# Pinned instruction order, operand tiles made ahead and moved pools in a hybrid decoder layer

## The chip, the cores and the metric

The kernel runs on one core of one Trainium2 chip. The metric is the device time of one launch in microseconds (us); the median of three runs of the kernel before is 2411.76 (2410.3 to 2414.46). TensorE (PE) multiplies matrices, PEld is its weight load, VectorE (DVE), ScalarE (ACT) and GpSimd (POOL) work on elements, SyncE (SP) starts loads. Each engine takes its instructions in the order in which they are queued.

## The reference

One decoder layer over 2048 tokens of 1024 features, all in float32; `D_FF` is 2816.

```python
h = rms_norm(x, g_mix[i])
proj = h @ w_in[i]
u, v, qk, vm, o, ig, fg = jnp.split(proj, cuts, axis=-1)
gm = gmlp_mixer(u, v, gm_ln_g[i], gm_ln_b[i], gm_ws[i], gm_bs[i])      # 8 heads, chunks of 128 tokens
qk = jax.nn.silu(causal_dwconv(qk, ml_conv_w[i], ml_conv_b[i]))
q, k = jnp.split(qk, 2, axis=-1)
ml = mlstm_mixer(q, k, vm, ig + ml_b_i[i], fg + ml_b_f[i], o, ml_norm_g[i])   # 4 heads, chunks of 128
x = x + jnp.concatenate([gm, ml], axis=-1) @ w_out[i]
h = rms_norm(x, g_ffn[i])
up = causal_dwconv(h @ w_up[i], ffn_conv_w[i], ffn_conv_b[i])
a, bv = jnp.split(up, 2, axis=-1)
x = x + (jax.nn.silu(a) * bv) @ w_down[i]
gate = jax.nn.sigmoid(rms_norm(x, g_ple[i]) @ w_ple_gate[i])
x = x + gate * (p[i] @ w_ple[i])
# after the layer: rms_norm(x, g_final)
```

## The kernel before

**Products.** Every large float32 product is made from operands that are split into a high part and the remainder, both in the type fp32r: high by high, high by low, low by high, so three matmuls for each pair of tiles. `wsplit`, `split` and `halves` make the parts: ScalarE copies the high part, VectorE subtracts it to get the low one. Features lie on the partitions and tokens along them.

**Mixer.** Four blocks of 512 tokens (`b` from 0 to 3). In a block `tok_group(0)` to `tok_group(3)` make the columns with tokens on the partitions (gates, v, o), `chain1` to `chain3` the running sums and maxima of the mLSTM gates, `qk_tile` the eight convolved tiles of q and k (steps `u`, `cv`, `qk`), `head_a`, `head_b` and `head_out` the mLSTM heads one after another (`hc` is scaled by `sr` at L588 to L591, transposed into `tr` at L598, and written to `cat`), `u_tile` and `mix` the gMLP heads. `out_first` starts two tiles of the output projection between the steps of the last head; the other six follow, 24 matmuls each, and each tile is added to `xr` (the input) and stored to `x1s`. While that runs, `split` makes the `h` of the next block from `hf` (L683), 8 times; the last block has none.

**Side work.** VectorE has work in the mixer that serves the channel mixer. `ffn_in` normalizes a finished block and stores it, and sums of it, to the DRAM tiles `tds`; `sums_make` (L261 on) adds and subtracts parts of `w_down` that `sums_load` has brought into the two tiles `ds0` and `ds1`, and stores the results to `sds`. In the program text most `sums_make` stand in the loop over output tiles, four of them in the last block.

**Channel mixer.** Two halves of 1024 tokens. Both its products use a scheme of seven products of half-size blocks in place of eight, in the order `ORDER = (1, 2, 6, 5, 7, 3, 4)`. `Up` makes 22 column tiles (`j`) from the tiles `T[prod, kk]`, 4 for each of the seven products, 28 in all, which `build_t` loads from `tds` and splits during `j = 0`; for the second half `load_t` and `make_t` do it during `Down`. `Down` (L940 to L1016) takes 11 steps for each product; its `load` (L952, L953) brings weights and activations into slots `x`, `prep` splits them (`dw`, `dt`, L770 and L771), `fetch` (L962) brings residuals that are needed when a product is complete. `sums` of `Up` (L912) stores the sums of activations that `Down` reads. A list of steps gives each load and each split a lead: `(4, load)` is issued four steps ahead of the matmuls that need it.

**Last stage.** `Ple` runs four blocks of gate products (`gt`, `gs`) with its weights loaded by `load4` (L1035) during the second `Down`. The last block goes in two halves of 256 tokens. For each, `q1` sums the squares by small matmuls and takes the root, `q2` spreads the scale `dgf` over the tokens (L203), and `emit_half` (L1130) multiplies the eight tiles by it and stores them.

**Order.** Loads are issued by SP, stores by POOL (two weight loads at the start by ACT). The framework chooses the order of each engine's instructions by a model of its own, so an instruction of later work may be queued ahead of what stands before it in the text. `tc.keep_in_program_order` (in `keep`) ties an instruction behind the one that was traced before it on the same engine. On-chip memory is handed out by pools in the order in which these are opened; `SLOTS` gives the tags of the channel mixer's slots, `(count, columns)`.

## Time and profile before

| | |
|---|---|
| median of the runs | 2411.76 us |
| profiled execution | 2413.49 us, span 2411.8, mean granted clock 0.99 |
| busy: PE / DVE / ACT / POOL | 2347.6 (97%) / 1814.7 (75%) / 1106.5 (46%) / 206.3 (9%) |
| mixer blocks 0 to 3 end at | 228.9, 448.7, 663.7, 884.6 us |
| first half: `Up` ends, `Down` ends | 1318.8, 1534.0 us |
| second half: `Up` ends, `Down` ends | 1956.1, 2147.0 us |
| `Ple` | 264.8 us, to the end of the span |

Busy time is the time in which an engine executes an instruction; the span runs from the first to the last recorded instruction, and the execution's own time is a little longer than the span. PE's busy share by stage goes from 94% (block 0, 216.02 of 228.90) to nearly 100% (second `Up`, 421.04 of 422.10). The granted clock is the share of TensorE's full speed that the chip gave in a stretch.

### The profile page before, as it was taken

Reading aid. Unit: us, or ns where it says so; the run is one execution under the profiler, and the core shown is the slowest. Engines: PE = TensorE matmul, PEld = TensorE weight load, DVE = VectorE, ACT = ScalarE, POOL = GpSimd, SP = SyncE. Lnnn points to the kernel's source line nnn. Section 1 sums busy time; section 2 is a strip of 40 time slices with the busy share of each in tenths; the row PEclk is TensorE's granted clock in tenths of the full one; section 3 lists DMA queues with packets and bytes.
Section 4 is the critical chain, followed back from the end, with each engine's and each line's share of the span. In section 5 each row is a group of like instructions: output and inputs, shape, how many; then the busy total and the mean of one; then the engine's idle time right before and its main releaser. Section 6 shows DMA issues by size and latency. Waiting matters only on the chain.

```text
span 2411.8 us, 31443 instructions
## 1 busy us (share of the span) xinstructions
PE 2347.6 (97%) x11336; PEld 1992.5 (83%) x11336; DVE 1814.7 (75%) x3107; ACT 1106.5 (46%) x1850; POOL 206.3 (9%) x339
## 2 busy tenths in 40 slices
PE   8999999999999989999999999999999999999998
PEld 8888977998798868878888788888888878888887
DVE  7787678668756859888988566888888866575665
ACT  4453266246315635444444565544444445553223
POOL 1000110011211100011100000010000000000000
PEclk9999999999999999999999999999999999999998
DMA  7426452644556454345435787332323368671112
GB/s 251 132 70 202 131 183 84 205 140 149 202 174 202 139 209 153 136 148 179 141 109 179 262 292 236 130 116 101 109 101 117 117 221 300 210 261 45 70 70 71
DMA packets 148413, 382.73 MB, mean 159 GB/s; under 512 B 17696, under 2 KB 19872, under 8 KB 148256
## 3 DMA queue, kind: packets, MB, share of 16 engines
q1 hardware_dynamic: 121872, 291.16, 37.1%
q0 software_dynamic: 26240, 89.15, 9.5%
q8 instruction: 89, 1.46, 0.2%
q14 instruction: 68, 0.56, 0.1%
q10 hardware_dynamic: 144, 0.40, 0.1%
HBM read 283.12 MB, written 97.52 MB: 158 GB/s over the span
## 4 chain that ended last, share of the span: by engine, by line
PE 81%; DVE 7%; DMA 6%; issue 3%; ACT 1%; POOL 1%; SPq 0%; DVEq 0%; POOLq 0%; ACTq 0%
PE ub L864 6%; PE ub L865 6%; PE ub L866 6%; PE ua L864 4%; PE ua L865 4%; PE ua L866 4%; PE acc L125 3%; PE acc L126 3%; PE gt L125 3%; PE gt L126 3%; PE gt L128 3%; PE da L977 3%; PE acc L128 3%; PE da L978 3%; PE da L976 3%; PE acc L369 3%
## 5 line engine op out<-in xcount | busy, mean ns | idle before, releaser
L864 PE MATMUL ub<-tt,sw 128*128 128x512 f32 x704 | 275.3, 392 | 7.4 <-ACT tt L770 4.6
L865 PE MATMUL ub<-tt,sw 128*128 128x512 f32 x704 | 275.2, 391 | 2.8 <-DVE tt L771 2.8
L866 PE MATMUL ub<-tt,sw 128*128 128x512 f32 x704 | 274.6, 390 | 0.0
L776 ACT ACTIVATE sw<-wr 128x1024 fp32r<-128x1024 f32 x132 | 140.1, 1061 | 289.2 <-PE ua L865 247.2
L864 PE MATMUL ua<-tt,sw 128*128 128x512 f32 x528 | 206.0, 390 | 0.0
L865 PE MATMUL ua<-tt,sw 128*128 128x512 f32 x528 | 205.9, 390 | 0.0
L866 PE MATMUL ua<-tt,sw 128*128 128x512 f32 x528 | 205.7, 390 | 0.0
L771 DVE TENSOR_TENSOR dt<-sx,dt 128x512 fp32r<-128x512 f32 x154 | 106.4, 691 | 105.1 <-ACT dt L770 104.8
L369 PE MATMUL acc<-whi,hh 128*128 128x384 f32 (+1 forms) x512 | 174.1, 341 | 8.5 <-ACT hh L218 7.0
L118 DVE TENSOR_TENSOR wlo<-wst,whi 128x1024 fp32r<-128x1024 f32 (+2 forms) x144 | 158.4, 1103 | 24.9 <-ACT whi L114 15.9
L370 PE MATMUL acc<-wlo,hh 128*128 128x384 f32 (+1 forms) x512 | 173.5, 339 | 2.6 <-DVE wlo L118 2.6
L371 PE MATMUL acc<-whi,hl 128*128 128x384 f32 (+1 forms) x512 | 173.0, 339 | 0.2 <-DVE hl L219 0.2
L777 DVE TENSOR_TENSOR sw<-wr,sw 128x1024 fp32r<-128x1024 f32 x132 | 161.2, 1221 | 15.1 <-ACT sw L776 12.3
L864 PEld LDWEIGHTS ub<-tt,sw 128*128 128x128 f32 x704 | 132.5, 188 | 38.5 <-ACT tt L770 5.5
L770 ACT ACTIVATE dt<-sx 128x512 fp32r<-128x512 f32 x154 | 96.9, 629 | 135.3 <-PE db L978 73.9
L865 PEld LDWEIGHTS ub<-tt,sw 128*128 128x128 f32 x704 | 132.7, 188 | 30.9 <-DVE tt L771 3.6
L866 PEld LDWEIGHTS ub<-tt,sw 128*128 128x128 f32 x704 | 132.7, 189 | 27.5
L976 PE MATMUL da<-dt,dw 128*128 128x512 f32 x352 | 137.0, 391 | 7.1 <-ACT dt L770 7.1
L977 PE MATMUL da<-dt,dw 128*128 128x512 f32 x352 | 138.1, 392 | 0.3 <-DVE dt L771 0.2
L978 PE MATMUL da<-dt,dw 128*128 128x512 f32 x352 | 137.7, 391 | 0.0
L114 ACT ACTIVATE whi<-wst 128x1024 fp32r<-128x1024 f32 x80 | 84.2, 1058 | 93.0 <-PE acc L371 35.2
L771 DVE TENSOR_TENSOR dw<-sx,dw 128x512 fp32r<-128x512 f32 x154 | 105.7, 686 | 24.2 <-ACT dw L770 24.2
(341 smaller groups left out, 5766.8 us busy)
## 6 DMA issues: line engine op xcount, KB each, us to landing
wr<-w_up SPq DMA_DIRECT2D x44, 512.0 KB, 3.6
wr<-w_up SPq DMA_DIRECT2D x88, 256.0 KB, 4.8
act<-fc POOLq DMA_DIRECT2D x44, 512.0 KB, 5.8
ad<-two POOLq DMA_DIRECT2D x88, 256.0 KB, 4.9
sx<-sd SPq DMA_DIRECT2D x88, 256.0 KB, 3.8
sx<-ad SPq DMA_DIRECT2D x88, 256.0 KB, 4.0
wst<-w_v SPq DMA_DIRECT2D x48, 384.0 KB, 3.4
sx<-w_down SPq DMA_DIRECT2D x66, 256.0 KB, 4.1
```

What stands on the lines that cost most here:

```text
L118: (leng or V).tensor_tensor(lo[:, :n], st[:, :n], hi[:, :n].bitcast(F32), ALU.subtract)
L369: PE.matmul(ps[t][:, :n], a_h, rh, start=(k == 0), stop=False)
L370: PE.matmul(ps[t][:, :n], a_h, rl, start=False, stop=False)
L371: PE.matmul(ps[t][:, :n], a_l, rh, start=False, stop=(k == KD - 1))
L771: keep(V.tensor_tensor(t[:, HALF:], x, t[:, :HALF].bitcast(F32), ALU.subtract), pin)
L777: keep(V.tensor_tensor(lo, x, hi.bitcast(F32), ALU.subtract), pin)
L864: PE.matmul(ps, hi[:, c], t[:, :HALF], start=first, stop=False, skip_group_check=on)
L865: PE.matmul(ps, hi[:, c], t[:, HALF:], start=False, stop=False, skip_group_check=on)
L866: PE.matmul(ps, lo[:, c], t[:, :HALF], start=False, stop=last, skip_group_check=on)
L976: PE.matmul(ps, w[:, c], t[:, :HALF], start=first, stop=False, skip_group_check=on)
L977: PE.matmul(ps, w[:, c], t[:, HALF:], start=False, stop=False, skip_group_check=on)
L978: PE.matmul(ps, w[:, HALF + d * 128:HALF + (d + 1) * 128], t[:, :HALF], start=False, stop=last, skip_group_check=on)
```

## The change

The edits, in the order of the diff:
- Slots `k` are divided into `kp` (12) and `k` (16). `kp` and the temporary and persistent pools of the mixer get places of their own: `big` and the new pool `pre` lie on the other side of the memory, `sm` and `tp` are opened earlier, tiles of 320 and 96 bytes (`GAP_W`, `GAP_P`) are put between, each tag of slots has its own pool. `xr` of the mixer has three buffers in place of two.
- The first weight load and the first load of the input are made in two halves each, and the first splits too.
- `keep` is put on VectorE instructions: `hf`, the first operation of `sums_make`, those of `ffn_in`, the scale in `q1`, `dgf` in `q2`, the products of `emit_half`; and on SP's loads in `load_t`, `fetch`, `load4` and `Ple.load`.
- The 12 tiles `T` of products 1, 2 and 6 of the first half are loaded and split during the last output projection (`pre_load`, `pre_make`); the other 16 are built as before, with a lead of 3 steps in place of 8.
- The last `sums` of an `Up` half uses slots `m` in place of `x`.
- In the end the first half's `emit_half` is cut in two, with the second half's `q2` between.

```diff
-SLOTS = {"k": (28, 1024), "r": (7, 1024), "f": (4, 1024), "w": (2, 3072), "m": (8, 512), "x": (4, 1024)}
+SLOTS = {"kp": (12, 1024), "k": (16, 1024), "r": (7, 1024), "f": (4, 1024), "w": (2, 3072), "m": (8, 512), "x": (4, 1024)}
+GAP_W, GAP_P = 80, 24
...
-    big = mx.enter_context(tc.tile_pool(name="mbig", bufs=1))
-    hpool = mx.enter_context(tc.tile_pool(name="hpool", bufs=2))
+    bx = ExitStack()
+    big = bx.enter_context(tc.tile_pool(name="mbig", bufs=1, side="right"))
+    hpool = mx.enter_context(tc.tile_pool(name="hpool", bufs=1))
...
+    sm = mx.enter_context(tc.tile_pool(name="msmall", bufs=2))
+    tp = mx.enter_context(tc.tile_pool(name="mtmp", bufs=2))
+    gap = mx.enter_context(tc.tile_pool(name="gap", bufs=1))
+    gap.tile([P, GAP_W], F32, name="gap")
...
+    dpool = mx.enter_context(tc.tile_pool(name="dpool", bufs=1))
+    cpool = mx.enter_context(tc.tile_pool(name="cpool", bufs=1))
...
-    def hpair(nm):
-        hi = hpool.tile([P, KD, TB], F32R, tag="hh", name=nm + "h")
-        lo = hpool.tile([P, KD, TB], F32R, tag="hl", name=nm + "l")
+    def hpair(nm, pool):
+        hi = pool.tile([P, KD, TB], F32R, tag="hh", name=nm + "h")
+        lo = pool.tile([P, KD, TB], F32R, tag="hl", name=nm + "l")
...
-    A.dma_start(w_raw[:, :2 * GW[0]], w_v0[0])
+    for i in range(2):
+        c = slice(i * GW[0], (i + 1) * GW[0])
+        A.dma_start(w_raw[:, c], w_v0[0][:, c])
...
+    def keep(ins, pin=True):
+        if pin:
+            tc.keep_in_program_order(ins)
...
-            V.tensor_scalar(r, mp[:, :nt], 1.0 / D, EPS, ALU.mult, ALU.add)
+            keep(V.tensor_scalar(r, mp[:, :nt], 1.0 / D, EPS, ALU.mult, ALU.add))
...
         def q2(self):
...
-            V.tensor_tensor(dg.rearrange("p (c t) -> p c t", t=128),
+            keep(V.tensor_tensor(dg.rearrange("p (c t) -> p c t", t=128),
...
-                            self.r.rearrange("p (c o) -> p c o", o=1).broadcast_to([P, nt, 128]), ALU.mult)
+                            self.r.rearrange("p (c o) -> p c o", o=1).broadcast_to([P, nt, 128]), ALU.mult))
...
-            V.scalar_tensor_tensor(xs[:, i, :], xs[:, i, :], c1(C_GFFN + kk + 4 * i), rB, ALU.mult, ALU.mult)
+            keep(V.scalar_tensor_tensor(xs[:, i, :], xs[:, i, :], c1(C_GFFN + kk + 4 * i), rB, ALU.mult, ALU.mult))
...
-        V.tensor_tensor(t7, xs[:, 1, :], xs[:, 0, :], ALU.subtract)
+        keep(V.tensor_tensor(t7, xs[:, 1, :], xs[:, 0, :], ALU.subtract))
...
+    T, raw_t, PRE = {}, {}, (1, 2, 6)
+    def pre_load(prod, kk):
+        raw_t[prod] = xpool.tile([P, 2, TB], F32, tag="xs", name="xs")
+        DMA.dma_start(raw_t[prod], tds[0][prod][:, kk:kk + 2, :])
+    def pre_make(prod, kk, pool):
+        for i in range(2):
+            t = pool.tile([P, 1024], F32R, tag="kp", name="tt", bufs=SLOTS["kp"][0])
+            A.activation(t[:, :TB], raw_t[prod][:, i, :], AF.Copy)
+            V.tensor_tensor(t[:, TB:], raw_t[prod][:, i, :], t[:, :TB].bitcast(F32), ALU.subtract)
+            T[prod, kk + i] = t
...
     def ds_tile(i):
-        return big.tile([P, 2, TB], F32, tag=f"ds{i}", name=f"ds{i}")
+        return dpool.tile([P, 2, TB], F32, tag=f"ds{i}", name=f"ds{i}")
...
     def sums_make(k):
...
-        V.tensor_tensor(q[:, 1, :], p[:, 1, :], q[:, 1, :], ALU.add)
+        keep(V.tensor_tensor(q[:, 1, :], p[:, 1, :], q[:, 1, :], ALU.add))
...
-        tp = mx.enter_context(tc.tile_pool(name="mtmp", bufs=2))
-        sm = mx.enter_context(tc.tile_pool(name="msmall", bufs=2))
...
         def mssq():
...
-        h = hpair("h")
+        h = hpair("h", hpool)
...
+        w_first = [wpool.tile([P, 1024], F32R, tag=t, name=t) for t in ("whi", "wlo")]
+        def first_half(i):
+            c = slice(i * GW[0], (i + 1) * GW[0])
+            V.tensor_copy(w_first[0][:, c], w_raw[:, c])
+            V.tensor_tensor(w_first[1][:, c], w_raw[:, c], w_first[0][:, c].bitcast(F32), ALU.subtract)
...
+            if k0 == 0:
+                first_half(0)
+                for c in (slice(0, TB // 2), slice(TB // 2, TB)):
+                    DMA.dma_start(xs[:, 0, c], xT[0, :, 0, c])
+                for c in (slice(0, TB // 2), slice(TB // 2, TB)):
+                    A.activation(h[0][:, 0, c], xs[:, 0, c], AF.Copy, scale=c1(C_GMIX))
+                    V.scalar_tensor_tensor(h[1][:, 0, c], xs[:, 0, c], c1(C_GMIX), h[0][:, 0, c].bitcast(F32), ALU.mult, ALU.subtract)
+                nq.add(xs[:, 0, :])
+                first_half(1)
+                continue
...
-            if k0 == 0:
-                w_first = wsplit(None, 2 * GW[0], V, V, w_raw)
...
-            cat = hpair("cat")
+            cat = hpair("cat", cpool)
...
+            if b + 1 == NB:
+                bx.close()
+                pre = ctx.enter_context(tc.tile_pool(name="pre", bufs=1, side="right", reuse_waits="tile"))
+                pre.tile([P, SLOTS["kp"][1]], F32, tag="kp", name="kp", bufs=SLOTS["kp"][0])
+                pre.tile([P, GAP_P], F32, name="gap")
+                todo = [(prod, kk) for prod in PRE for kk in (0, 2)]
...
-                hn = hpair("h")
+                hn = hpair("h", hpool)
...
                 def split(k, x):
...
-                    V.scalar_tensor_tensor(f, x, c1(C_GMIX + k), nx.rB, ALU.mult, ALU.mult)
+                    keep(V.scalar_tensor_tensor(f, x, c1(C_GMIX + k), nx.rB, ALU.mult, ALU.mult))
...
-                xr = tp.tile([P, TB], F32, tag="xr", name="xr")
+                if b + 1 == NB:
+                    if 2 <= d:
+                        pre_make(*todo[d - 2], pre)
+                    if 1 <= d <= 6:
+                        pre_load(*todo[d - 1])
+                xr = tp.tile([P, TB], F32, tag="xr", name="xr", bufs=3)
...
-        U = fx.enter_context(tc.tile_pool(name="slots", bufs=1, reuse_waits="tile"))
+        U = {t: fx.enter_context(tc.tile_pool(name=f"slots_{t}", bufs=1, reuse_waits="tile")) for t in "wxrkfm"}
+        U["kp"] = pre
...
         def slot(tag, nm, dt=F32):
...
-            return U.tile([P, size], dt, tag=tag, name=nm, bufs=n)
+            return U[tag].tile([P, size], dt, tag=tag, name=nm, bufs=n)
...
         def build_t(s, prod, kk):
...
-            T[prod, kk] = halves(raw_t[prod][:, kk % 2, :], "k", "tt")
+            T[prod, kk] = halves(raw_t[prod][:, kk % 2, :], "kp" if prod in PRE else "k", "tt")
...
         def load_t(s, prod, kk):
...
-            DMA.dma_start(raw_t[prod, kk], tds[s][prod][:, kk, :])
+            keep(DMA.dma_start(raw_t[prod, kk], tds[s][prod][:, kk, :]))
...
         def make_t(prod, kk):
-            T[prod, kk] = halves(raw_t.pop((prod, kk)), "k", "tt", True)
+            T[prod, kk] = halves(raw_t.pop((prod, kk)), "kp" if prod in PRE else "k", "tt", True)
...
             def sums(self):
...
-                one = Twos()
+                one = Twos() if self.j < NJ - 1 else (lambda: slot("m", "two"))
...
             def fetch(self, fh, th):
...
-                    DMA.dma_start(self.x[q], x1s[2 * self.s + th][:, 4 * fh + 2 * q:4 * fh + 2 * q + 2, :])
+                    keep(DMA.dma_start(self.x[q], x1s[2 * self.s + th][:, 4 * fh + 2 * q:4 * fh + 2 * q + 2, :]))
...
             def snap(self, bank):
...
-                    t = pairs(slot("k", "sn"))
+                    t = pairs(slot("kp" if self.s else "k", "sn"))
...
         def load4(key, src, tag="r"):
...
-            DMA.dma_start(raw_w[key], src)
+            keep(DMA.dma_start(raw_w[key], src))
...
-                    DMA.dma_start(self.xp[-1], x2s[i][:, d:d + 2, :])
+                    keep(DMA.dma_start(self.xp[-1], x2s[i][:, d:d + 2, :]))
...
             def start(self, ds=range(KD), pin=False):
...
-                    h = slot("k", "hg", F32R)
+                    h = slot("kp", "hg", F32R)
...
-        def emit_half(o, fin, lo, hi):
-            for k in range(0, KD, 2):
+        def emit_half(o, fin, lo, hi, ks=range(0, KD, 2)):
+            for k in ks:
...
-                    V.tensor_tensor(x, x, fin.rB, ALU.mult)
+                    keep(V.tensor_tensor(x, x, fin.rB, ALU.mult))
...
-                ex.setdefault((0, prod), []).append((8, lambda prod=prod, kk=kk: build_t(0, prod, kk)))
+                if prod not in PRE:
+                    ex.setdefault((0, prod), []).append((3, lambda prod=prod, kk=kk: build_t(0, prod, kk)))
...
-            emit_half(ple[b], fa, 0, TB // 2)
+            emit_half(ple[b], fa, 0, TB // 2, (0, 2))
...
+            emit_half(ple[b], fa, 0, TB // 2, (4, 6))
...
```

## Rows read from the trace of the kernel before

**Rows 1.** The head of the page.

```profile
span 2411.8 us, 31443 instructions
```

**Rows 2.** Windows: length, busy us (count) by engine, granted clock, DMA share, GB/s.

```profile
186.00:198.00 12.00, 9.21 (x36) 7.10 (x35) 11.22 (x28) 5.38 (x13) 1.01 (x1) 0.86 0.36 111
...
325.00:335.00 10.00, 5.89 (x36) 4.34 (x34) 7.78 (x12) 5.74 (x11) 2.16 (x4) 0.83 0.66 236
...
672.00:679.00 7.00, 4.42 (x17) 4.09 (x16) 6.05 (x11) 0.63 (x1) 2.52 (x4) 0.76 0.58 200
...
838.00:882.00 44.00, 44.00 (x205) 36.43 (x204) 17.88 (x42) 9.66 (x19) 4.84 (x8) 1.00 0.39 128
...
882.00:903.00 21.00, 13.56 (x44) 9.83 (x43) 18.15 (x26) 14.56 (x24) 0.54 (x1) 0.84 0.85 310
...
1329.00:1338.00 9.00, 5.36 (x16) 3.70 (x15) 2.86 (x5) 3.19 (x6) 0.07 (x1) 0.81 0.98 360
...
1400.00:1500.00 100.00, 100.00 (x443) 82.80 (x442) 61.94 (x95) 56.41 (x96) 1.07 (x2) 1.00 0.80 268
...
1966.00:1975.00 9.00, 5.29 (x21) 3.42 (x21) 2.72 (x5) 3.04 (x5) 0.21 (x1) 1.00 0.96 347
```

**Rows 3.** Waits of PE: instruction, releaser, us in all, times, longest.

```profile
PE acc L598 <- DVE hc L591: 10.7, 5, 2.8
...
PE pm L554 <- ACT qk L546: 10.4, 5, 3.9
...
PE da L976 <- ACT dt L770: 7.1, 2, 3.6
...
PE acc L369 <- ACT hh L218: 7.0, 2, 6.3
```

**Rows 4.** Timeline of DVE, 186 to 200 us: start, length, line, what.

```profile
190.41 0.74 DVE L683 SCALAR_TENSOR_TENSOR hf<-xs,col,rB 128x512 f32<-128x512 f32 x1
...
192.42 0.87 DVE L591 TENSOR_SCALAR hc<-hc,sr 128x128 f32<-128x128 f32 x4 [0.27 <-POOL sr L588]
```

**Rows 5.** Timeline of DVE, 320 to 336 us; in brackets the idle time before.

```profile
324.57 0.69 DVE L261 TENSOR_TENSOR ds<-ds,ds 128x512 f32<-128x512 f32 x1 [4.04 <-DMA ds<-w_down]
```

**Rows 6.** Timeline of DVE, 882 to 903 us.

```profile
886.94 3.69 DVE L771 TENSOR_TENSOR tt<-hx,tt 128x512 fp32r<-128x512 f32 x6
```

**Rows 7.** DMA issues: engine, count, KB each, median us from issue to landing.

```profile
ds<-w_down SPq DMA_DIRECT2D x22, 512.0 KB, 5.0
...
sd<-ds POOLq DMA_DIRECT2D x44, 256.0 KB, 2.5
...
xs<-xT SPq DMA_DIRECT2D x2, 256.0 KB, 4.2
...
col<-cols SPq DMA_DIRECT2D x1, 134.0 KB, 3.6
```

**Rows 8.** Timeline of SP's queue and of ACT, 1318 to 1340 us.

```profile
1325.73 0.32 SPq L962 DMA_DIRECT2D xr<-x1s  x1
...
1332.13 0.63 ACT L770 ACTIVATE dw<-sx 128x512 fp32r<-128x512 f32 x1 [8.00 <-DMA sx<-w_down]
```

**Rows 9.** Timeline of ACT, the first 12 us.

```profile
5.48 0.72 ACT L218 ACTIVATE hh<-xs,col 128x512 fp32r<-128x512 f32 x1 [2.76 <-DMA xs<-xT]
```

**Rows 10.** Timeline of DVE, the last 16 us.

```profile
2398.75 0.42 DVE L203 TENSOR_TENSOR dgf<-ident,nr 128x256 f32<-128x256 f32 x1
2399.32 0.42 DVE L150 TENSOR_TENSOR sq<-sq 128x256 f32<-128x256 f32 x1
...
2401.21 2.40 DVE L1130 TENSOR_TENSOR xg<-xg,bank 128x256 f32<-128x256 f32 x7
2403.52 0.42 DVE L203 TENSOR_TENSOR dgf<-ident,nr 128x256 f32<-128x256 f32 x1
```

**Rows 11.** Lines of PE, shapes apart: tiles, shape, count, busy, mean ns, idle before.

```profile
L864 PE MATMUL ua<-tt,sw 128*128 128x512 f32 x528 | 206.0, 390 | 0.0
...
L166 PE MATMUL bank<-sh,onesr 128*128 128x512 f32 x8 | 3.2, 406 | 0.0
```

More of the change, by code (lines that the diff above doesn't have):

```diff
@@ L762, in __call__ @@
                 return self.t[:, (self.i - 1) % 2, :]
-        def keep(ins, pin=True):
-            if pin:
-                tc.keep_in_program_order(ins)
         def halves(x, tag, nm, pin=False):
@@ L803, in trunk_kernel @@
         steps = Steps()
-        T = {}
-        raw_t = {}
         def build_t(s, prod, kk):
```

## The prediction

> **What bounds the kernel now.** I read the page first, then the view of waits for TensorE (PE), then busy time by stage, and the timeline of each queue around the stalls. The profiled execution spans 2411.8 us [rows 1]; its own time is 2413.49, so 1.7 us lie outside the span, and the median of the runs is 2411.76, 1.7 below it. I take the sum off the profiled time and then 1.7 more. In an undisturbed stretch 443 matmuls take 100 us, 0.226 us each [rows 2], and nothing in the diff changes their number or shape. So only the stretches in which PE does less than that can give time back. The view of waits shows how few they are: PE waits 10.7 us for `hc` in `head_out`, 10.4 for `qk`, 7.1 for `dt`, 7.0 for the first `hh` [rows 3]. Behind most of these stands one pattern: an instruction of later work has been placed early in an in-order queue and holds up what PE needs.
>
> What each stretch loses is its length less its matmuls at 0.226 us [rows 2]:
> - 186 to 198: 36 matmuls, 8.1 us, so 3.9 lost. The three longest waits for `hc` are alike (near 189, 409 and 624), so 11.6 in all.
> - 325 to 335: here many matmuls are short, so I count the wait and the clock. The longest wait for `qk` is 3.9 us [rows 3], and the granted clock of 0.83 over 10 us takes another 1.7 [rows 2]: 5.6. A second stretch like it stands near 763; five such waits make 10.4, so it can hold at most 6.5; I take 3.5 and the same 1.7: 5.2.
> - 672 to 679: 17 matmuls, 3.8 us, so 3.2.
> - 882 to 903, the first tiles of the channel mixer: 44 matmuls, 9.9 us, so 11.1.
> - 1329 to 1338 and 1966 to 1975, the start of each `Down`: 16 and 21 matmuls, 3.6 and 4.7 us, so 5.4 and 4.3.
>
> Together 46.4 us. The clock belongs to it: before each drop PE had stood still for some us, so a wait that goes takes its slow stretch with it.
>
> **The change, part by part.**
>
> *Pinned VectorE (DVE) operations.* At 190.41 DVE runs `hf` of the next block's split (0.74 us) ahead of the `sr` and `hc` steps, and `hc` comes at 192.42 [rows 4]. `keep` on that `hf` puts it behind the last `catl` of `head_out`. What it loses is cover for the split: 8 times `hf` and `hl` must then run within the output projection, but there DVE is busy 17.9 of 44 us [rows 2], so it costs nothing while those 26 us are free. The last block has no split and no such wait. I leave 0.5 us in each place: gain 10.
>
> *Pinned sums.* At 324.57 DVE starts `sums_make`, after 4.04 us of waiting for `ds` [rows 5]; the `cv` steps behind it feed `qk`. In program order these sums stand in the output projection. The same line stands behind the stretches at 672 and 763. Of 5.6 + 5.2 + 3.2 = 14.0 I count 12. The moved work is not free in the last block: there four `sums_make` of four operations (about 0.69 each, 11 us) and the 12 new tile subtractions (0.61 each [rows 6], 7.4 us) come to the 17.9 us in 44, 36 in all: it fits. But one `sums_make` (2.8 us), its store (2.5) and the next load (5.0 [rows 7]) make 10.3 us, against two output tiles of 24 matmuls, 10.8 us. If a load is late, DVE waits with all that follows: between 0 and 4.0 us each for three loads. Since the medians just fit and PE's low-part products come last in each tile, I take 2 us.
>
> *Tiles made ahead.* Twelve of 28 `T` tiles are now made in the output projection, into a pool of their own. Before, six subtractions run from 886.94 on, after the projection has ended, and PE waits for them [rows 6]. DVE is busy 18.15 of the 21 us there [rows 2]. Less 7.4 that leaves 10.8, still a little more than the 9.9 that PE needs; with one late `sums_make` in it, 13.5. So 0.9 to 3.6 us stay, I take 2.5, and the gain is 8.6. Twelve ScalarE copies of about 0.6 us move along; ScalarE was busy 9.7 of 44 us in the projection [rows 2].
>
> *Pinned loads, and the last sums in `m` slots.* At 1325.73 SP issues `fetch` (`xr`), a load that is needed far later, and only behind it the `sx` loads; ScalarE then waits 8.0 us for `w_down` until 1332.13 [rows 8]. Pinned, `fetch` stands behind the loads of its own step, and `load4` likewise at 1962. The last `sums` leave the `x` slots to these loads. Queued behind a pinned load are all later loads of SP, but each has a lead of four steps, 48 matmuls or 10.8 us. I count 8.7 of 9.7. If `x` slots alone had been the limit, the second edit would do it by itself.
>
> *First loads in halves.* The first `hh` takes 0.72 us and waits 2.76 us for `xs` [rows 9]; half of it saves 0.36. A transfer of 256 KB lands in 4.2 us here and one of 134 KB in 3.6 [rows 7], so half a load gains at most 0.6, and nothing if both halves share the queue. Between 0 and 1.0 I take 0.5. The Trainium skill (SBUF — State Buffer, The DMA setup-cost knee) says that a transfer pays about 2 us whatever its size and advises one large transfer instead of several; by its rate the first half would land an estimated 0.3 us earlier, and with the copy's 0.36 the sum would be 37.0 in place of 36.8. The 3.6 us for 134 KB agree with a large fixed part.
>
> *The end.* Seven products of the first half run from 2401.21, 2.40 us, and the second `dgf` starts only at 2403.52 [rows 10]. Four products (1.4 us) ahead of it put it 0.8 us earlier. But the pin also ties the first half's `dgf`, which now runs at 2398.75, behind the last `sq` sum, which starts at 2399.32 and takes 0.42 [rows 10]: 1.0 us later, and the products with it. If PE takes the four small matmuls of `q1` in that time, 0.2 of the 0.8 stay; if they queue behind the later scale, 0.4 us are lost. Between -0.4 and 0.8 I take 0.
>
> *Moved pools.* `xr` with a third buffer and the order of the pools cost no instruction. Whether they cost pace depends on addresses. The small and temporary pools are 3648 and 41088 bytes; the gap of 320 makes 45056, 88 times 512, so weights keep their place against `h` and `cat`. I take it that the 96 bytes do so for the tiles on the other side.
>
> Sum: 10 + 12 + 8.6 + 8.7 + 0.5 + 0 = 39.8, less 2 for late sums and 1 for waits that appear elsewhere: 36.8. 2413.5 - 36.8 - 1.7 = 2375.
>
> **The rivals.**
> - *A bottleneck moves in (23%).* Work that was spread over the mixer is pressed into the last projection and the first tiles, and DVE is short there. Then the entry gives only 3 us, the last block loses 5 more, and pinned operations wait for loads in two or three other places, 4 us each. For it: 86% DVE in the entry. Against: 26 free us in the projection. 39.8 less 5.6, 5 and 10 is 19.2: 2393.
> - *Slower by alignment (6%).* If the gaps miss, operands lie apart as `sh` and `onesr` do, whose matmuls take 406 ns against 390 [rows 11]. Those in the new tiles, 3 of 7 products in 44 tiles, 1584 matmuls, would cost up to 25 us, and all 9000 or so up to 144. From 2300 matmuls at 16 ns on, the 36.8 us are gone; with half of all, 72 us lost, it is 2447. The difference of 16 is a mean of 8 with another operand form, so it is an upper bound. The Trainium skill (SBUF — State Buffer, Who interferes with whom) says that PE never waits on its two read ports; by that this case would cost nothing and have no chance. No run here shows the layout moved yet, so I keep it.
> - *The pins do nothing (5%).* A pin ties an operation only to the one traced before it; if that one is early too, the order stays. Then the entry's gain is lost to late sums, and the time is within 0.2% of 2411.8.
>
> **How the numbers follow.** The forecast, 2375, has 66%, with 2363 to 2387 as its own range. Rival one reaches 2400. With all 46.4 and 1 at the start it would be 2364, and some of PE's smaller waits may go too, so the low end is 2355; the high end, which leaves out the alignment and the pins that do nothing, is 2402. 0.2%, about what a measurement can tell from no change, is 5 us: faster 0.89, same 0.05, slower 0.06.
>
> **What would show it.** Right: no wait of PE for `hc` over 1 us; no DVE `sums_make` that waits in the middle of a block; PE's first `ub` within 1 us of the last output matmul and 44 matmuls in about 13 us; no drop of the clock at either `Down`; `dgf` of the second half between products, with the last instruction within 0.5 us of its old distance from the last matmul of `gt`. Wrong: a matmul pace other than 0.226 us; DVE over 95% from 838 to 900 with PE waiting for `wlo` or `tt`; SP blocked on a pinned load while PE waits for `dt`.

## The result, and where the time went

The changed kernel takes 2399.09 us in the median (2393.97 to 2400.68, four runs), the kernel before 2411.16 beside it. The ratio of the runs is 0.9937 with a 95% interval from 0.9923 to 0.9952: faster by 0.6%, 12 us between the medians and 15 by the ratio, where 36.8 were forecast. The profiled execution is the fastest of the four, at 2393.97, so the stage lengths below flatter the change by some 5 us.

Each column holds stage lengths in us: from the first matmul of one stage to the first of the next, in the trace of that kernel. The names after "changed" are those of the experiments.

| stage | before | changed | e1 | e2 | e3 | e6 | e8 | e10 | e12 |
|---|---|---|---|---|---|---|---|---|---|
| block 0 | 222.7 | 219.0 | 221.5 | 218.9 | 221.8 | 218.1 | 218.0 | 221.3 | 217.5 |
| block 1 | 219.8 | 213.1 | 217.5 | 211.1 | 213.9 | 214.5 | 209.7 | 218.1 | 210.1 |
| block 2 | 215.0 | 219.5 | 227.1 | 218.3 | 219.5 | 217.0 | 216.3 | 222.8 | 218.3 |
| block 3 | 220.9 | 212.6 | 216.5 | 215.0 | 214.2 | 216.6 | 214.3 | 224.4 | 211.7 |
| first `Up` | 434.2 | 440.1 | 438.1 | 426.3 | 440.1 | 433.6 | 438.5 | 442.0 | 433.6 |
| block 3 and first `Up` | 655.1 | 652.7 | 654.6 | 641.3 | 654.3 | 650.2 | 652.7 | 666.4 | 645.3 |
| first `Down` | 215.2 | 209.4 | 209.4 | 209.4 | 209.4 | 209.4 | 209.4 | 209.4 | 209.4 |
| second `Up` | 422.0 | 422.0 | 421.6 | 422.9 | 423.3 | 421.7 | 421.6 | 422.8 | 421.7 |
| second `Down`, to the first gate product | 190.0 | 185.5 | 185.4 | 185.4 | 185.5 | 185.4 | 185.4 | 185.4 | 185.4 |

A wait in front of the first matmul of `Up` counts to block 3, so these two stages are also given together. What a block shows by itself is uncertain by some us: the kernel of e11, in which every engine has the same order as in the changed one, has 217.6, 214.8, 217.2 and 218.2 us in the four blocks.

Both starts of `Down` gave what was hoped for, blocks 0, 1 and 3 gained, but block 2 lost 4.5 us and the first `Up` half 5.9. The waits of PE after, in the form of [rows 3], show what is gone and what came:

```profile
PE ub L910 <- DVE sw L825: 12.2, 1, 12.2
PE acc L409 <- ACT vm L420: 6.1, 3, 2.8
PE acc L638 <- DVE hc L631: 5.6, 5, 1.8
PE acc L409 <- ACT hh L320: 5.6, 1, 5.6
PE bank L221 <- DVE dgf L217: 5.1, 2, 3.1
PE ub L908 <- DVE xr L756: 2.5, 1, 2.5
...
PE pm L594 <- ACT qk L586: 2.1, 3, 0.8
```

Against [rows 3], `hc` fell from 10.7 to 5.6 us, `qk` from 10.4 to 2.1, `hh` from 7.0 to 6.2 (5.6 here and 0.6 at L232, which was the same line before); `dt` is no longer in the list. In their place stands one wait of 12.2 us for a weight split `sw` in the entry of the channel mixer, and 6.1 us for `vm` that were 0.8 in the list of before. VectorE around the long one, in the timeline after:

```profile
853.71 0.69 DVE L288 TENSOR_TENSOR ds<-ds,ds 128x512 f32<-128x512 f32 x1 [2.79 <-DMA ds<-w_down]
...
860.51 0.68 DVE L756 TENSOR_TENSOR xr<-xr,acc 128x512 f32<-128x512 f32 x1
866.90 0.69 DVE L288 TENSOR_TENSOR ds<-ds,ds 128x512 f32<-128x512 f32 x1 [5.71 <-DMA ds<-w_down]
...
870.16 0.68 DVE L756 TENSOR_TENSOR xr<-xr,acc 128x512 f32<-128x512 f32 x1
880.28 0.69 DVE L288 TENSOR_TENSOR ds<-ds,ds 128x512 f32<-128x512 f32 x1 [9.43 <-DMA ds<-w_down]
...
882.34 1.22 DVE L825 TENSOR_TENSOR sw<-wr,sw 128x1024 fp32r<-128x1024 f32 x1
```

VectorE is idle for 9.43 us in front of the last `sums_make` (its first operation is L288 now), and the split that PE wants is queued behind. The window of the stretch, with the columns of [rows 2]:

```profile
866.00:888.00 22.00, 7.33 (x22) 5.10 (x21) 10.41 (x14) 1.54 (x3) 5.40 (x10) 0.61 0.71 270
```

VectorE is busy 10.41 of 22 us: it is not short of time but blocked. The granted clock is 0.61 in the mean of this window: it fell to its lower level (0.50, 1.2 GHz) at the end of the wait of 2.5 us for `xr` and rose again 3.2 us after the wait of 12.2 had ended. At 0.226 us each, 22 matmuls need 5.0 of the 22 us; of the 17 that are lost, 14.7 are the two waits and some 2 the clock. The Trainium skill (Perfetto Trace Analysis, Tensor Engine Instruction) calls VectorE and ScalarE strict FIFO; this row agrees.

### The profile page after: what moved, and what is told of

Read it like the earlier page. It is cut to its first block, busy times and chain, and to the rows that moved or that the text cites. A ratio compares the mean times of both kernels' runs of the same rounds, so it can differ in the third digit from the quotient of the medians.

```text
span 2392.2 us, 31472 instructions
## 1 busy us (share of the span) xinstructions
PE 2335.7 (98%) x11336; PEld 1985.1 (83%) x11336; DVE 1815.1 (76%) x3110; ACT 1105.3 (46%) x1851; POOL 199.9 (8%) x339
## 4 chain that ended last, share of the span: by engine, by line
PE 81%; DMA 6%; DVE 6%; issue 4%; ACT 1%; POOL 1%; SPq 0%; POOLq 0%; DVEq 0%; ACTq 0%
PE ub L908 6%; PE ub L910 6%; PE ub L909 6%; PE ua L909 4%; PE ua L908 4%; PE ua L910 4%; PE da L1020 3%; PE da L1021 3%; PE da L1022 3%; PE gt L139 3%; PE gt L142 3%; PE gt L140 3%; PE acc L409 3%; PE acc L410 3%; PE acc L411 3%
## 5 line engine op out<-in xcount | busy, mean ns | idle before, releaser
L910 PE MATMUL ub<-tt,sw 128*128 128x512 f32 x704 | 274.3, 390 | 12.2 <-DVE sw L825 12.2
L409 PE MATMUL acc<-whi,hh 128*128 128x384 f32 (+1 forms) x512 | 175.6, 343 | 13.4 <-ACT vm L420 6.1
```

Of the source, the lines that this page charges most:

```text
L409: PE.matmul(ps[t][:, :n], a_h, rh, start=(k == 0), stop=False)
L910: PE.matmul(ps, lo[:, c], t[:, :HALF], start=False, stop=last, skip_group_check=on)
```

## The experiments

Ratios are to the kernel before on the same chip; differences between two kernels are taken from the ratios, times 2412 us, and each ratio is uncertain by some 0.2%, 5 us, a difference of two ratios by some 6. Where a stage tells more, the table above is used.

**e1: the first operation of `sums_make` without its pin.**

```diff
-        keep(V.tensor_tensor(q[:, 1, :], p[:, 1, :], q[:, 1, :], ALU.add))
+        V.tensor_tensor(q[:, 1, :], p[:, 1, :], q[:, 1, :], ALU.add)
```

> The changed kernel without the pin on the first operation of sums_make; nothing else differs. In the built order three of the sums move forward again (two into block 1's token groups, one into block 2's heads); the last one stays ahead of the first weight split of the channel mixer. Theory A (the stall of PE of 12.2 us at the entry is the round of make, store and load through the one pair of ds tiles): the entry stays as it is, 12 us of waiting and the slow clock behind it, and the first Up half stays near 440 us; blocks 1 and 3 lose 3 to 5 us each to waits for qk, as the kernel before did, so 2397 to 2408. Rival B (the pin holds VectorE at the entry): the stall at the entry goes, the Up half falls to about 426 us, and the time is 2383 to 2392.

2408.32 us (2405.89 to 2413.21), ratio 0.999 (0.998 to 1.0). All four blocks lose, 18.4 us together, and the entry stays: PE still waits 9.2 us there and the first `Up` half takes 438.1. The longest waits of PE in e1:

```profile
PE ub L910 <- DVE sw L825: 9.2, 1, 9.2
PE acc L409 <- ACT vm L420: 8.8, 3, 4.0
PE acc L638 <- DVE hc L631: 7.4, 6, 2.8
```

The pin earns its place, and it isn't what blocks the entry: rival B falls. The losses came by `vm`, `hc` and one wait of 4.4 us for `xr`, not by the waits for `qk` that I expected: these stay at 2.1 us, as in the changed kernel. Without the pin the sums do not go back to where they stood before the change, so e1 doesn't show what took the waits for `qk` away.

**e2: loads of the last block's sums into the free `h` tiles.**

```diff
+                spare = [hpool.tile([P, KD, TB], F32, tag=t, name="dsx") for t in ("hh", "hl")]
...
+                        n = turn[d + 2] - 7
+                        sums_load(turn[d + 2], lambda i: spare[i][:, 2 * n:2 * n + 2, :])
```

> The changed kernel; the four sums of the last block's output projection load into parts of the two h tiles, which are free there, so that no load waits for a store of the sums before it. The arithmetic, its place and the twelve tiles made ahead are the same. Theory A (the round through one pair of ds tiles makes the sums late): the waits of VectorE for w_down of 2.8, 5.7 and 9.4 us go, the 12.2 us wait of PE goes with the 17 us of half clock, and the first Up half falls from 440 to 424 to 428 us; time 2380 to 2387. Rival B (VectorE has too much to do around the entry): VectorE is then busy without a gap from the last heads on, PE still waits 6 us or more for sw or wlo, and the time is 2392 to 2399.

2382.28 us (2380.35 to 2386.59), ratio 0.9887 (0.9865 to 0.9908), 12 us better than the changed kernel. No wait of VectorE for the sums' `w_down` is left in that stretch, and the first `Up` half takes 426.3 us, 13.8 less, or 11.4 less with block 3. Theory A holds: the round of make, store and load through one pair of tiles was late. A smaller wait of PE came instead, in front of the first matmul of `Up`; here it is in the views of waits of e2, of PE and of SP's queue:

```profile
PE ub L913 <- ACT sw L829: 6.9, 2, 6.0
```

```profile
SPq L878 <- DMA sd<-dsx: 9.4, 1, 9.4
```

The first `w_up` load is issued at 863.48 (at 813.59 in the changed kernel), since its slot lies in the memory that the sums now occupy: SP stands 9.4 us in front of it until the stores `sd` have ended.

**e3: `hf` without its pin.**

```diff
-                    keep(V.scalar_tensor_tensor(f, x, c1(C_GMIX + k), nx.rB, ALU.mult, ALU.mult))
+                    V.scalar_tensor_tensor(f, x, c1(C_GMIX + k), nx.rB, ALU.mult, ALU.mult)
```

> The changed kernel without the pin on hf. Theory C (the pin on hf gave back what it won: the split of the next block's h ends later, the xs tiles and the square sums behind it come later, and PE waits 2.9 and 3.2 us for the copies of vm in blocks 1 and 2): the waits for hc of about 3 us come back in blocks 0 to 2 (10 us with the slow clock), the waits for vm at the ends of the first token groups of blocks 1 and 2 go (9 us with the slow clock), and the time is the same within 4 us: 2395 to 2402. Rival D (the waits for vm have another cause, the sums or the loads of xr): they stay, and the time is 2405 to 2411.

2399.63 us (2396.43 to 2402.3), ratio 0.9952 (0.9934 to 0.997). The two waits of PE trade places, in the view of waits of e3:

```profile
PE acc L638 <- DVE hc L631: 14.7, 6, 4.3
...
PE acc L409 <- ACT vm L420: 1.3, 2, 0.8
```

The pin on `hf` is worth 9.1 us of `hc` and costs 4.8 us of `vm`, plus the slow clock behind either. The four blocks are 5.2 us longer without it and the ratio is 3.6 us higher, neither clear of the uncertainty, so the pin alone is worth between 0 and some 5 us. The expectation was right in place; it put both prices about equal, and `hc` is the larger.

**e4: three `xs` tiles.** Room for them came from `xr` (two buffers, as before the change) and the temporary tiles.

```diff
-    xpool = mx.enter_context(tc.tile_pool(name="xpool", bufs=2))
+    xpool = mx.enter_context(tc.tile_pool(name="xpool", bufs=3))
-NQ, NT = 5, 8
+NQ, NT = 5, 7
-                xr = tp.tile([P, TB], F32, tag="xr", name="xr", bufs=3)
+                xr = tp.tile([P, TB], F32, tag="xr", name="xr", bufs=2)
```

> The changed kernel with three xs tiles in place of two; to make room, xr has two buffers in place of three and the temporary tiles are seven in place of eight. Theory C (late xs tiles): the waits for vm at the ends of the first token groups of blocks 1 and 2 fall from 2.9 and 3.2 us to under 1, the time is 2388 to 2395. Rival D (w_down loads queued ahead of xs, or xr loads that hold ScalarE, delay the squares): the waits stay within 1 us of what they were, 2396 to 2403.

2420.19 us (2417.9 to 2422.66), ratio 1.0034 (1.0019 to 1.0048): slower than before. PE now waits 15.2 us for `xr`. Neither theory had this. The wait for `vm` is down to 0.5 us, but it is 0.8 in e10 too, which has two `xs` tiles: PE now stands for `xr` just before. So e4 says nothing on `xs`; e10 takes up `xr`.

**e5: three edits undone, each in its stage.**

```diff
-                one = Twos() if self.j < NJ - 1 else (lambda: slot("m", "two"))
+                one = Twos() if self.j < NJ - 1 or self.s == 0 else (lambda: slot("m", "two"))
...
-            keep(DMA.dma_start(raw_w[key], src))
+            DMA.dma_start(raw_w[key], src)
...
-            keep(V.tensor_tensor(dg.rearrange("p (c t) -> p c t", t=128),
+            V.tensor_tensor(dg.rearrange("p (c t) -> p c t", t=128),
```

> The changed kernel with three edits undone, each in a stage of its own: the last sums of the first half use x slots again (fetch stays pinned), load4 is not pinned (the slots m stay in the second half), dgf in q2 is not pinned. Theory E (at each start of Down both edits are needed): the first Down goes from 209.4 to 212 to 215 us, with a wait of PE for dt of 2 to 4 us. Rival F (the pin on fetch alone does it): the first Down stays at 209.4 within 0.5. The second Down goes from 185.4 to 189 to 190 us without the pin on load4 (theory E), or stays (rival F: the slots alone do it). At the end my prediction took 0 for the pin: last product to end of span within 0.5 us of the changed kernel's; if the pin costs its full 1 us there, that much is gained. Together 2402 to 2409 by E, 2398 to 2401 by F on both.

2396.1 us (2393.89 to 2398.19), ratio 0.9929 (0.9914 to 0.9943), the same as the changed kernel. The first `Down` takes 210.5 us, 1.1 more: of the 5.8 us won there the `m` slots have about 1, the rest is there with the pin on `fetch` alone. The second `Down` is the same, 185.4 us, without the pin on `load4`. From the gate products that follow the last `Down` matmul to the last matmul, and from there to the end of the span, it is 0.9 us shorter (232.9 + 6.6 against 233.4 + 7.05): without the pin `dgf` stands ahead of the last `sq` sum again. The same stretch was 234.2 + 6.6 before the change, so the pin costs 0.9 us of the 1.3 that the other edits there gain. VectorE's timeline of e5:

```profile
2385.00 0.42 DVE L217 TENSOR_TENSOR dgf<-ident,nr 128x256 f32<-128x256 f32 x1
2385.57 0.42 DVE L164 TENSOR_TENSOR sq<-sq 128x256 f32<-128x256 f32 x1
```

**e6: as e2, but all 28 `T` tiles built after the projection, with the old lead of 8.** The calls of `pre_load` and `pre_make` are taken out.

> The kernel with the ds space of the h tiles, but all 28 T tiles are built after the projection, with a lead of 8 steps as before the change. Theory G (the tiles made ahead are worth the 8.6 us that the prediction gave them, and the late sums hid it): the first Up half goes from 426.3 to 433 to 436 us, the time to 2388 to 2393. Rival H (with the sums out of the way the tiles are no bottleneck): 426 to 429 us, and 2380 to 2385.

2388.49 us (2387.43 to 2390.09), ratio 0.9898 (0.9883 to 0.9913). The first `Up` half is 7.3 us longer than in e2 (433.6 against 426.3), 8.9 with block 3, and PE waits 12.8 us for `tt`. Theory G holds in the stage; by the ratios the tiles are worth only 3 us, with 6 of uncertainty.

**e7: two pairs of tiles for the last sums.** Sums 7 and 9 in `ds`, 8 and 10 in one free `h` tile.

```diff
+                spare = hpool.tile([P, KD, TB], F32, tag="hl", name="dsx")
...
+                    if b + 1 == NB and turn[d + 2] % 2 == 0:
+                        n = turn[d + 2] // 2 - 4
+                        sums_load(turn[d + 2], lambda i: spare[:, 4 * n + 2 * i:4 * n + 2 * i + 2, :])
```

> The changed kernel; sums 7 and 9 of the last block use the ds tiles, 8 and 10 one free h tile, so that each load can start while the other pair is worked on, and the memory in which the first w_up slot lies is not used. Theory A (the round through one pair is what is late): no wait of VectorE for w_down over 3 us in the last block, no wait of PE over 2 us at the entry, the first Up half 421.5 to 425 us, the time 2375 to 2381. Rival I (the loads are late because the DMA engines are full there, whatever the buffers): the last sums still wait 5 us or more, and PE waits 5 us or more for sw: 2384 to 2395.

2388.62 us (2386.63 to 2391.09), ratio 0.9895 (0.9878 to 0.9911). The sums aren't late any more, as A said, but the half takes 435.9 us: PE waits 6.6 us for the first `T` tile that is not made ahead (views of waits of e7, of PE and of SP's queue).

```profile
PE ua L913 <- ACT tt L823: 6.6, 1, 6.6
```

```profile
SPq L878 <- DMA sd<-dsx: 10.1, 3, 8.9
```

Its load (`hx`) is issued only at 877.80, behind a `w_up` load at 876.47, in front of which SP stood 8.9 us for the stores of the last sums. The time lies in the range of rival I, but its signs (late sums, 5 us or more of waiting for `sw`) are absent: the cause was right, and the next late load took half of it (block 3 and the half take 647.1 us, between the 641.3 of e2 and 652.7).

**e8: the next block's squares behind the gate steps.**

```diff
-                stream(xT[b + 1], lambda k, x: nx.add(x))
+                stream(xT[b + 1], lambda k, x: nx.add(x, b > 0 and k < 2))
```

`add` passes the second argument to `keep` for its square and its sum.

> The changed kernel with the first two squares of the next block's norm, and the sum of them, pinned behind the gate steps of the first token group in blocks 1 and 2, so that the copies of gt and vm stand ahead of all squares on VectorE and ScalarE; hf stays pinned. Theory C (the copies of vm come late because the squares stand ahead of them and wait for xs): the waits for vm of 2.9 and 3.2 us fall under 1, hc stays under 2, block 1 goes from 213.1 to about 210 us and block 2 from 219.5 to about 215; time 2389 to 2394. Rival J (the squares are then late for the norm in the third token group): PE waits 3 us or more for sh or the gates of VectorE in blocks 1 and 2; 2396 to 2404.

2391.44 us (2385.97 to 2395.63), ratio 0.9908 (0.9888 to 0.9928), 7 us better than the changed kernel. No wait for `vm` is left among the longest; block 1 falls to 209.7 us (209.6 and 210.1 in e9 and e12, which have this edit too), block 2 to 216.3, but it takes 218.3 in e12 with the same edit, so that gain isn't clear. In the changed kernel the chain that delays `vm` is seen in the timelines of VectorE, first, and ScalarE:

```profile
451.67 0.69 DVE L164 TENSOR_TENSOR sq<-sq 128x512 f32<-128x512 f32 x1 [3.43 <-ACT sq L162]
...
458.27 0.23 DVE L424 SCALAR_TENSOR_TENSOR gt<-acc,col 128x8 f32<-128x8 f32 x2
```

```profile
451.00 2.44 ACT L162 ACTIVATE sq<-xs 128x512 f32<-128x512 f32 x4 [5.80 <-DMA xs<-xT]
458.46 1.10 ACT L420 ACTIVATE vm<-acc 128x384 f32<-128x384 f32 x2 [5.02 <-DVE gt L424]
```

The squares wait 5.80 us for `xs`, the sums and the weight splits follow, and only then, from 458.27 on, the copies that free PE's accumulators. Theory C holds for the waits; the 7 us of the ratio are hardly clear of their uncertainty.

**e10: `xr` with two buffers, all else as changed.**

```diff
-                xr = tp.tile([P, TB], F32, tag="xr", name="xr", bufs=3)
+                xr = tp.tile([P, TB], F32, tag="xr", name="xr", bufs=2)
```

> The changed kernel with two xr buffers as before the change, all else the same. My prediction gave the third buffer no effect: same time within 3 us. Rival L (with the sums pinned into the projection VectorE adds the output tiles late, and with two buffers the next xr load is late as well, so that the output tiles' PSUM is not released; the run with three xs tiles, which had two xr, waited 15 us for xr): waits of PE for xr of 4 us or more at the ends of blocks 0 to 2 and at the entry, time 2405 to 2415.

2418.18 us (2411.82 to 2421.43), ratio 1.0017 (1.0008 to 1.0027), 19 us worse than the changed kernel and no better than before. Rival L holds, as the view of waits of e10 shows:

```profile
PE acc L409 <- DVE xr L756: 16.5, 5, 5.2
PE ub L910 <- DVE sw L825: 13.2, 1, 13.2
...
PE ub L908 <- DVE xr L756: 5.8, 1, 5.8
```

At the end of block 1 the `xr` load of the seventh of the eight output tiles is issued at 448.15, just behind a load of the pinned sums. What it waited for is its buffer: the store of the fifth tile, issued at 442.86 among the stores of the sums, takes 5.2 us to land. The load takes 5.2 more, and VectorE waits in front of a tile whose accumulator PE wants (waits of SP's queue from 436 to 452 us, its timeline, and the timeline of VectorE in e10):

```profile
SPq L755 <- DMA x1s<-xr: 10.3, 4, 6.5
```

```profile
447.72 0.33 SPq L280 DMA_DIRECT2D ds<-w_down  x1
448.15 0.40 SPq L755 DMA_DIRECT2D xr<-xT  x1
```

```profile
453.40 0.69 DVE L756 TENSOR_TENSOR xr<-xr,acc 128x512 f32<-128x512 f32 x1 [5.40 <-DMA xr<-xT]
```

**e11: gaps of 64 and 32 bytes.** The order on every engine is unchanged.

```diff
-GAP_W, GAP_P = 80, 24
+GAP_W, GAP_P = 16, 8
```

> The changed kernel with the two gaps at 64 and 32 bytes in place of 320 and 96; the order of instructions on every engine is the same. The weight tiles of the mixer then lie 256 bytes, the new T tiles 64 bytes away from their place against the other operands. The prediction's rival on alignment: up to 16 ns on each of the some 4500 matmuls of the mixer with such weights and the 1584 with new T tiles, 25 to 97 us in all, the pace of the acc matmuls with 512 columns rises from 226 ns to up to 242. Against it: pace and time stay the same, 2394 to 2403.

2399.19 us (2397.61 to 2404.94), ratio 0.9949 (0.9937 to 0.9962): the same as changed. In the mixer, with its weights 256 bytes off, 46 matmuls fit into 10 us in both kernels. In the second `Up` half, with the new tiles 64 bytes off, there are 440 in 100 us (windows of e11, columns as in [rows 2]):

```profile
1600.00:1700.00 100.00, 100.00 (x440) 82.17 (x439) 83.14 (x110) 45.11 (x53) 8.67 (x16) 1.00 0.32 108
```

against 442 in the window of the changed kernel:

```profile
1600.00:1700.00 100.00, 100.00 (x442) 82.79 (x442) 85.88 (x115) 46.02 (x54) 8.63 (x16) 1.00 0.32 109
```

That half takes 424.7 us in e11, and 421.6 to 423.3 in the other kernels. From start to start a matmul of it takes 227 ns in the median of every product in the changed kernel; in e11 it takes 229 to 230 in products 1, 2 and 6, which read the shifted tiles, 231 in product 5, whose tiles lie in slots `k` and were not shifted, and 227 in the other three. The gate products of `Ple`, which read shifted tiles too, go from 227 to between 229 and 231.

**e9 and e12: the repairs together.** e9 is two pairs as in e7 (8 in the upper, 10 in the lower half of the `h` tile), the squares of e8, and `dgf` without its pin. e12 turns the pairs round (7 and 9 in the `h` tile, 8 and 10 in `ds`).

> Three repairs together: two pairs of tiles for the sums of the last block (8 in the upper, 10 in the lower half of the free h tile, so that the x slots come free first), the squares of the next norm pinned behind the gate steps, and dgf in q2 without its pin. If the three causes are the right ones and independent (theories A and C, and the pin at the end): block 1 near 209.7 us, block 2 near 216.3, the first Up half 422 to 427 with no wait of PE over 2.5 us at the entry, the end 0.9 us shorter than the changed kernel's; time 2370 to 2377. Rival K (another load takes the place at the entry again, as the first T tiles did with two pairs before): Up half 432 us or more, 2380 to 2387.

2381.02 us (2379.53 to 2383.76), ratio 0.9868 (0.9854 to 0.9881). Blocks 1 and 2 (209.6 and 216.4 us) and the end came as expected, the first `Up` half didn't: 435.2, with 8.1 us of waiting for `tt`, whose load again came behind a `w_up` load that the stores of the last sums held back (SP stood 8.5 us for them). Rival K.

> The three repairs, with the pairs changed round: sums 7 and 9 in the free h tile, 8 and 10 in the ds tiles, so that the last stores touch neither the second w_up slot nor the x slots of the first T tiles. If it is the slots' memory that held SP's loads behind the last sums (the 8.1 us wait for the first T tile in the run before), the second w_up load and the hx loads are issued before the projection ends, no wait of PE at the entry is over 3 us, the first Up half takes 422 to 427 us and the whole 2369 to 2375. If the DMA engines are what is short there, another load is late by 5 us or more: Up half 430 us or more, 2377 to 2383.

2379.08 us (2377.23 to 2380.02), ratio 0.9855 (0.9838 to 0.9871): the fastest of all, 1.45% better than before and 20 us better than the change. But the half still takes 433.6 us, as in the second branch of the expectation; now a `w_up` load is late, and the split that PE waits 7.0 us for, at 870.03, stands on VectorE behind the operation that needs this load (timeline of VectorE in e12, and waits of SP's queue from 840 to 870 us):

```profile
865.58 0.69 DVE L891 TENSOR_TENSOR wr<-wr 128x512 f32<-128x512 f32 x1 [7.06 <-DMA wr<-w_up]
```

```profile
SPq L760 <- DMA x1s<-xr: 12.2, 2, 7.3
```

The three loads of that tile were issued from 855.30 to 856.66, and the last took 8.8 us to land. Before them SP had stood 12.2 us in front of two `xr` loads, until the stores of earlier `xr` tiles ended: even the three buffers bind here. Whether a fourth, a better order on SP or only fewer bytes would end this is open.

## Why the prediction was wrong

The time lies in the range, near its upper end, but the gain is less than half of the forecast. In the traces the change gains 19.6 us (2411.8 less 2392.2): 10.3 at the starts of `Down`, where I had 8.7, but only 8.3 from block 0 to the end of the first `Up` half, where I had 27.6 (10 + 12 + 8.6, less 2 and 1). Step by step:

- **Late sums: the step that failed.** "Since the medians just fit [...], I take 2 us." I put one round of sums at 10.3 us from the medians of [rows 7] against 10.8 us for two output tiles. The rounds took 13.2 and 13.4 us (866.90 less 853.71, 880.28 less 866.90). Every term but one was longer than I took it: from the first operation to the last store's issue 3.6 us for 2.8, that store 3.2 and 5.1 for 2.5, the last load 6.2 and 4.5 for 5.0. The projection also carries the loads of the tiles made ahead; whether these made the transfers slower was not separated. Each round is so some 2.5 us longer than two output tiles, and VectorE fell behind PE with waits of 2.8, 5.7 and 9.4 us. I allowed 0 to 4.0 us for each of three loads, up to 12, and took 2 from medians that just fitted; that the lateness of one round passes to the next I did not count. Price, by e2: 12 us in the ratio, 11.4 in block 3 and the first `Up` half together.
- **The pin on `hf`: mis-sized.** I costed the moved split at nothing, since VectorE had 26 free us in the projection. Those were of the last block's, which has no split. In block 0, VectorE was busy 21.50 of 34 us of the projection before the change and 28.47 of 35 after it (windows below). It still fits, but the split holds the `xs` tiles, and the output tiles, sums and squares queue behind it. What comes late next is `vm`, in blocks 1 and 2. Forecast 10, alone 0 to 5 (e3), some 7 more once the squares stand elsewhere (e8). `hc` itself still has waits of 1.6 to 1.8 us, over the 1 us that I had named as the sign.
- **The third `xr` buffer: missed.** "`xr` with a third buffer [...] cost no instruction" is true, and without it the change gains nothing (e10, 19 us). I asked what the buffer costs and not what the pins would do to two.
- **Pinned sums:** forecast 12, by e1 13 in the ratio and 18.4 in the blocks. Right in size, but by luck: I had them free `qk`, and taking the pin away brings back `vm`, `hc` and `xr` instead. `qk` did fall from 10.4 to 2.1 us; which edit did that stays open.
- **Tiles made ahead:** forecast 8.6, by e6 7.3 in the half and 8.9 with block 3, though 3 by the ratios. Right in the stage, but hidden behind the late sums: the `Up` half ended longer than before.
- **Loads of `Down`:** forecast 8.7, measured 5.8 + 4.5. Right in sum; in the second `Down` it was not the pin on `load4` (e5), and which of the edits left there did it was not tried.
- **First loads:** PE starts at 5.57 in place of 6.26, 0.7 for the forecast 0.5. **The end:** 0.4 gained for 0; by e5 the pin lost 0.9, and the other edits there gained 1.3, where I had 0.8 for the cut.
- **The rivals.** What happened is the one called "a bottleneck moves in", forecast at 2393 with 23%: right about pinned operations that wait for loads, wrong that VectorE would be short at the entry, as it was idle there. Alignment was no loss here. Pins did move instructions, so the third fell.

The two windows of block 0's projection, first of the kernel before, then of the changed one (columns as in [rows 2]):

```profile
195.00:229.00 34.00, 34.00 (x146) 28.03 (x146) 21.50 (x30) 10.76 (x15) 3.84 (x7) 0.96 0.71 237
```

```profile
190.00:225.00 35.00, 35.00 (x156) 28.81 (x156) 28.47 (x42) 13.99 (x20) 5.62 (x10) 1.00 0.71 234
```

## What to carry to other kernels

A pin that moves work to its own place in the text also moves its loads, its stores and what these hold: before it is costed at nothing, follow each buffer round its whole circle (load, use, store, next load) and compare the circle under the traffic of that stretch with the beat of the loop; a circle that is 25% too long isn't late once but more each time. Count the free time in the stretch into which the work moves, not in one that lacks this work. Where an engine is idle and yet the bound, look at what is queued in front, not at its load. And when an edit looks free, like one more buffer, take it out of the finished kernel alone before calling it so.

## What was not expected of the hardware

A shift of one operand by 64 bytes slowed the fp32r matmuls that read it by 1 to 2% (227 to between 229 and 231 ns from start to start), one by 256 bytes not at all (46 in 10 us each). In `Up` three of seven products read the shifted tiles, but a fourth, product 5, slowed as well (231 ns), so the shift of a matmul's own operand isn't the whole account. The Trainium skill (SBUF — State Buffer, Who interferes with whom) gives PE two independent read ports and allows only the pair that VectorE and GpSimd share to contend; by that the shift would cost nothing. The pace differs by little, and where page and rows differ the rows stand, but what in the addresses does it was not tried.
